# A retrieval layer on one NeuronCore: sixteen more tokens by gathered score rows, another layout of the gate matrix, and work moved between two stages

## The chip, the cores and the metric

The kernel runs on one core of a Trainium2 chip. The metric is the device time of one execution in microseconds (us), as the median of several runs. One execution was profiled; times inside it count from the start of its span.

## The reference

Two layers, each with a mixer (not touched here) and a retrieval layer over 16,384 single-neuron experts, 8 heads with 16 experts each per token, 512 tokens of width 1024:

```
s1 = q[..., :half] . sub_keys[0];  s2 = q[..., half:] . sub_keys[1]
v1, i1 = top_k(s1, 16);  v2, i2 = top_k(s2, 16)
top, pos = top_k(v1[:, None] + v2[None, :], 16)      # 128 experts per token in all
eidx = cidx[pos];  gate = softmax(top)
act  = gelu(sum_d h[t, d] * expert_u[eidx[t, k], d])
y[t] = sum_k gate[t, k] * act[t, k] * expert_v[eidx[t, k], :]
```

## The kernel before

The 512 tokens are four tiles of 128. Three tiles (384 tokens, `DT`) are done densely: all 16,384 experts, in 128 chunks of 128, are scored for these tokens, and a matrix of gates that is zero nearly everywhere picks what counts. The fourth tile is done sparsely: for each of its 128 pairs a row of `peer_u` and one of `peer_v` is gathered per token by an indirect DMA from GpSimd's queue, with a dot product or a multiply-add on VectorE for each.

Of the dense tokens the last `MT` of the first tile in `TILES` are an exception: their columns are left out of the score matmuls, which are `DW = DT - MT` wide. Their scores come from gathered rows too (function `special`), `128 * MT / 128` gathers, each of 128 rows of 4 KB, and they are folded into the gate matrix, while the scores' place in `ga` is filled with ones.

A score chunk is `do_A`: 8 x 3 matmuls (L296 to L298) of the split weights `wh` and `wl` (float32 as a sum of two parts; ScalarE casts `wh`, L268, VectorE makes the remainder `wl`, L277) into one PSUM bank, then Gelu. `do_A` prepares the weights of chunks up to two ahead. The first `AHEAD` chunks are computed before the dense stage and stored in DRAM (`Sd`); the others are computed within it.

Per layer the stages that matter here are these.

- **One-hot stage** (L1106 to L1140): the gate matrix `Gd` is made for 384 tokens in 48 groups of 8 tokens (numbered 0 to 47 here). For a group VectorE writes one-hot rows (`onehots`, L1006 to L1009), TensorE multiplies them (16 matmuls of 128 columns, L1129 and L1130), ScalarE copies the result to `stg`. Every fourth group stores `stg` to `Gd`, 2 MB, from ScalarE's queue. VectorE's other work is spread between the groups: index lookups (`soh` tiles, L1391 to L1400), a step of `special`, and, by a planner, score chunks:

```
def fill(dve, pe=0.0):
    clk[0] += dve
    clk[1] += pe
    while clk[1] + 2.0 < clk[0] and done[0] < AHEAD - 5:
        do_A()
```

  `clk` holds planned times of VectorE and TensorE; `fill` adds a chunk where TensorE would run dry, up to five short of `AHEAD`. The last five follow after the loop.
- **Dense stage** (L1143 to L1270): per chunk a load of `peer_v`, its split `vh` and `vl` (L1165, L1166), the product of scores and gates (L1170), its split `whi` and `wlo`, and 18 matmuls of 512 columns (`vmul`, L1197 to L1202). Chunks with stored scores and chunks with fresh ones alternate; for the latter a `do_A` runs. The gates of 4 chunks come in one read `gtTrue` or `gtFalse` (old or fresh scores). The gathers of the fourth tile (`gather`, L1204 to L1232) go on beside, at a fixed number of rows per chunk: `u` rows of batch `bt` with `v` rows of batch `bt - 1`, 8 rows per batch.

Each engine's instructions run in the order in which the code issues them.

## Time and profile before

| | us |
|---|---|
| median of 3 runs | 2894.12 |
| lowest and highest run | 2890.52, 2898.0 |
| profiled execution | 2890.39 |
| its span | 2888.4 |
| TensorE matmul busy in the span | 2822.1 (98%) |
| VectorE busy | 2408.6 (83%) |
| ScalarE busy | 1286.3 (45%) |
| GpSimd busy | 950.2 (33%) |

A busy TensorE row says that matmuls were in flight, not that they were issued at the highest rate: they are pipelined, and the distance of two starts tells the rate. Names such as L296 are lines of the kernel before. `pa` and `pb` are PSUM banks, `grow` is a tile of gathered score rows, `row` one of the dense stage.

### The profile page before, as it was taken

To read this page: it belongs to the slowest core of one execution; us is meant where nothing else is said; L and a number is where in the kernel's file an instruction comes from. 1 tells how busy PE (TensorE), PEld (TensorE's weight loads), DVE (VectorE), ACT (ScalarE), POOL (GpSimd) and SP (SyncE) were. 2 spreads that over 40 slices of the span, in tenths; PEclk is the share of its full clock that TensorE was granted. 3 is DMA by queue.
4 is the path that set the end of the run, shared out by engine and by line. 5 is a ranking of instruction groups with operands and counts; after the bars stand their busy time and mean duration, and the time that the engine had idled before them with its cause. 6 is when DMAs were issued, how large, how long until landed. Compare 5 with 4: busy or idle time off the path is not lost. (4 is left out here: it accounts for less than half of the span.)

```text
span 2888.4 us, 41930 instructions
## 1 busy us (share of the span) xinstructions
PE 2822.1 (98%) x15203; PEld 2439.5 (84%) x15203; DVE 2408.6 (83%) x4724; ACT 1286.3 (45%) x2023; POOL 950.2 (33%) x809
## 2 busy tenths in 40 slices
PE   8999999999999999999999999999999999999999
PEld 4667899988888888888866778999888888888888
DVE  7868989978888888888868589899688888888887
ACT  4343466773333333333343434677633333333332
POOL 1424412003444433344323343120034443343442
PEclk9999999999999999999999999999999999999999
DMA  7443368779999999999944323687799999999996
GB/s 270 132 126 95 116 213 310 260 273 360 348 368 365 360 381 339 364 370 363 338 142 128 103 90 112 227 308 265 285 325 356 351 343 350 354 347 354 349 342 234
DMA packets 320272, 802.80 MB, mean 278 GB/s; under 512 B 27744, under 2 KB 157376, under 8 KB 316992
## 3 DMA queue, kind: packets, MB, share of 16 engines
q1 hardware_dynamic: 220144, 440.25, 45.2%
q0 software_dynamic: 78912, 285.41, 26.2%
q10 hardware_dynamic: 21008, 74.46, 6.8%
q8 instruction: 119, 1.95, 0.3%
q14 instruction: 89, 0.73, 0.1%
HBM read 723.42 MB, written 76.60 MB: 277 GB/s over the span
## 5 line engine op out<-in xcount | busy, mean ns | idle before, releaser
L296 PE MATMUL pa<-hh,wh 128*128 128x368 f32 (+1 forms) x2544 | 882.3, 347 | 4.5 <-ACT hh L371 1.9
L298 PE MATMUL pa<-hh,wl 128*128 128x368 f32 (+1 forms) x2544 | 869.4, 342 | 5.1 <-DVE wl L277 5.1
L297 PE MATMUL pa<-hl,wh 128*128 128x368 f32 (+1 forms) x2544 | 869.3, 342 | 3.1 <-DVE hl L364 2.7
L1166 DVE TENSOR_TENSOR vl<-vr,vh 128x1024 fp32r<-128x1024 f32 x256 | 313.3, 1224 | 257.4 <-ACT vh L1165 257.1
L296 PEld LDWEIGHTS pa<-hh,wh 128*128 128x128 f32 x2544 | 480.0, 189 | 43.2 <-issue 7.8
L297 PEld LDWEIGHTS pa<-hl,wh 128*128 128x128 f32 x2544 | 479.8, 189 | 29.3 <-DVE hl L364 4.5
L298 PEld LDWEIGHTS pa<-hh,wl 128*128 128x128 f32 x2544 | 479.0, 188 | 26.6 <-DVE wl L277 6.1
L1215 POOL DMA_INDIRECT row<-in_peer_u_dram,eidx x256 | 325.7, 1272 | 492.7 <-DVE acc L1228 363.8
L1165 ACT CAST vh<-vr 128x1024 fp32r<-128x1024 f32 x256 | 269.5, 1053 | 469.5 <-PE pb L1202 252.7
L1224 POOL DMA_INDIRECT row<-in_peer_v_dram,eidx x256 | 311.4, 1216 | 450.6 <-DVE row L1219 417.4
L268 ACT CAST wh<-wr 128x1024 fp32r<-128x1024 f32 x327 | 345.4, 1057 | 87.9 <-DMA wr<-in_peer_uT_dram 51.2
L277 DVE TENSOR_TENSOR wl<-wr,wh 128x1024 fp32r<-128x1024 f32 x266 | 325.6, 1227 | 33.9 <-PE pa L298 16.6
L1228 DVE SCALAR_TENSOR_TENSOR acc<-row,gw,acc 128x1024 f32<-128x1024 f32 x256 | 327.6, 1280 | 0.1
L1219 DVE SCALAR_TENSOR_TENSOR row<-row,htok 128x1024 f32<-128x1024 f32 x256 | 311.9, 1219 | 0.0
L1197 PE MATMUL pb<-vh,whi 128*128 128x512 f32 x762 | 300.0, 394 | 5.2 <-ACT whi L1174 5.1
L1199 PE MATMUL pb<-vl,whi 128*128 128x512 f32 x762 | 298.8, 392 | 0.0
L1200 PE MATMUL pb<-vl,whi 128*128 128x512 f32 x762 | 298.6, 392 | 0.0
L1202 PE MATMUL pb<-vh,wlo 128*128 128x512 f32 x762 | 297.6, 391 | 0.0
L1198 PE MATMUL pb<-vh,whi 128*128 128x512 f32 x762 | 297.4, 390 | 0.0
L1201 PE MATMUL pb<-vh,wlo 128*128 128x512 f32 x762 | 297.3, 390 | 0.1
L871 ACT ACTIVATE ga<-pa 128x368 f32<-128x368 f32 x256 | 122.6, 479 | 312.9 <-PE pa L298 310.8
L1132 ACT ACTIVATE stg<-pb 128x512 f32<-128x512 f32 x192 | 197.7, 1154 | 38.0 <-PE pb L1130 34.2
(335 smaller groups left out, 3923.8 us busy)
## 6 DMA issues: line engine op xcount, KB each, us to landing
wr<-in_peer_uT_dram SPq DMA_DIRECT2D x256, 512.0 KB, 7.5
vr<-in_peer_v_dram SPq DMA_DIRECT2D x256, 512.0 KB, 6.8
Gd<-stg ACTq DMA_DIRECT2D x24, 2048.0 KB, 8.6
adaw<-in_w_ada_dram SPq DMA_DIRECT2D x80, 512.0 KB, 4.4
gtFalse<-Gd SPq DMA_DIRECT2D x34, 768.0 KB, 12.8
Sd<-ga ACTq DMA_DIRECT2D x120, 192.0 KB, 4.3
gtTrue<-Gd SPq DMA_DIRECT2D x30, 768.0 KB, 10.7
gs<-Sd SPq DMA_DIRECT2D x120, 192.0 KB, 7.4
```

Of the source, the lines that this page charges most:

```text
L268: self.nc.scalar.copy(hi, raw)
L277: (eng or self.nc.vector).tensor_tensor(lo, raw, hi.bitcast(F32), ALU.subtract)
L296: nc.tensor.matmul(ps[:, :width], wh, hh[c][:, :width], start=c == first, stop=False)
L297: nc.tensor.matmul(ps[:, :width], wh, hl[c][:, :width], start=False, stop=False)
L298: nc.tensor.matmul(ps[:, :width], wl, hh[c][:, :width], start=False, stop=c == last)
L1166: nc.vector.tensor_tensor(vl, vr, vh.bitcast(F32), ALU.subtract)
L1197: nc.tensor.matmul(y0, a, vh[:, 0:512], start=f, stop=False)
L1199: nc.tensor.matmul(y0, a, vl[:, 0:512], start=False, stop=False)
L1215: nc.gpsimd.indirect_dma_start(out=r, out_offset=None, in_=A["peer_u"], in_offset=bass.IndirectOffsetOnAxis(ap=eidx[:, kk:kk + 1], axis=0))
L1219: nc.vector.scalar_tensor_tensor(r, r, 1.0, htok, ALU.mult, ALU.mult, accum_out=dots[:, k:k + 1])
L1224: nc.gpsimd.indirect_dma_start(out=r, out_offset=None, in_=A["peer_v"], in_offset=bass.IndirectOffsetOnAxis(ap=eidx[:, kk:kk + 1], axis=0))
L1228: nc.vector.scalar_tensor_tensor(acc, r, wb[bt - 1][:, k:k + 1], acc, ALU.mult, ALU.add)
```

## The change

- `MT` goes from 16 to 32: score matmuls are 352 columns wide instead of 368, and `special` gathers 32 rows instead of 16 per layer, two steps per group instead of one, with the same two buffers `grow`.
- `AHEAD` goes from 60 to 76; the planner's cost of a chunk on TensorE is now worked out from the width (3.84 instead of 4.2).
- `Gd` is stored as `[128, 32, 12, 128]` instead of `[12, 128, 128, 32]`: a read for 4 chunks is one run of 6 KB per partition instead of 12 of 512 bytes, and a store is 32 pieces of 512 bytes per partition instead of one of 16 KB.
- The first `NB0 * KB = 24` score rows of the fourth tile are gathered and multiplied in the one-hot stage (`early`, with three buffers: two `grow` and `H`) instead of the dense stage. For this the fourth tile's lookups move from the third to the second of the one-hot loop's tiles. In the dense stage `u` rows then run three batches ahead of the `v` rows.

```
-AHEAD = 60
-MT = 16
+AHEAD = 76
+MT = 32
+KB = 8
+NB0 = 3
...
-        Gd = self.dp.tile([DT // TB, P, NCHUNK, TB], F32, name=f"Gd{l}", tag="Gd")
+        Gd = self.dp.tile([P, NCHUNK // IG, DT // TB, IG * TB], F32, name=f"Gd{l}", tag="Gd")
...
-                        clk[1] += 4.2
+                        clk[1] += 24 * (DW / 2.4 + 13.3) * 1e-3
...
+                def early():
+                    n = NB0 * KB
+                    rows = []
+                    for k in range(n + 2):
+                        if k < n:
+                            rows.append(u([P, D], F32, "H") if k % 3 == 2 else grow())
+                            urow(k, rows[k])
+                        if k > 1:
+                            udot(k - 2, rows[k - 2])
+                            if (k - 1) % KB == 0:
+                                ugate((k - 1) // KB - 1)
+                            yield
...
-                    if k < 3 and next(spec, 0) is None:
-                        fill(1.3)
+                    for _ in range(2 if (n_ % 2 and NB0 * KB > 20) or MT > 16 else 1):
+                        if next(spec, 0) is None:
+                            fill(1.3)
...
-                        nc.scalar.dma_start(Gd[b0 // TB], stg)
+                        nc.scalar.dma_start(Gd[:, :, b0 // TB], stg.rearrange("p (a i) t -> p a (i t)", i=IG))
...
-                    nc.sync.dma_start(gts[old], Gd[:, :, i:i + IG, :].rearrange("b p i t -> p b i t"))
+                    nc.sync.dma_start(gts[old].rearrange("p b i t -> p b (i t)"), Gd[:, i // IG])
...
-                steps += 2.0 * NPAIR * (1 if i < AHEAD else 2) / (2 * NCHUNK - AHEAD - 6)
+                steps += (2.0 * NPAIR - NB0 * KB) * (1 if i < AHEAD else 2) / (2 * NCHUNK - AHEAD - 6)
```

`urow` issues a gather of one `peer_u` row per token, `udot` is its dot product with the tile's activations (`htok`), `ugate` applies Gelu and the gate to a batch of 8.

**Order, first place.** VectorE in the first part of layer 0's one-hot stage (group 7 of before); `oh` and `oi` are one-hots, `grow` a dot product of a gathered row, `wl` a remainder of the weights of a score chunk. Before:

```order
L1006 TENSOR_TENSOR oh_4070<-iota,ij_3470 128x1024
L1007 TENSOR_TENSOR oi_4071<-iota,ij_3470 128x1024
L1008 TENSOR_TENSOR oh_4070<-oi_4071,gg_3472 128x1024
L1009 TENSOR_TENSOR oh_4070<-oi_4071,gg_3472 128x1024
L1391 TENSOR_TENSOR soh_4076<-iotaA,ab_3282 128x2048
L1393 TENSOR_TENSOR soh_4076<-soh_4076,rep_4010 128x2048
L277 TENSOR_TENSOR wl_4084<-wr_4036,wh_4038 128x1024
L1056 SCALAR_TENSOR_TENSOR grow_4032,sdots_3301<-grow_4032,H_3302 128x1024
L277 TENSOR_TENSOR wl_4142<-wr_4080,wh_4082 128x1024
```

The same engine and stage with the change, a group that has a lookup as well:

```order
L1025 TENSOR_TENSOR oh_4268<-iota,ij_3472 128x1024
L1026 TENSOR_TENSOR oi_4269<-iota,ij_3472 128x1024
L1027 TENSOR_TENSOR oh_4268<-oi_4269,gg_3474 128x1024
L1028 TENSOR_TENSOR oh_4268<-oi_4269,gg_3474 128x1024
L1426 TENSOR_TENSOR soh_4274<-iotaA,ab_3284 128x2048
L1428 TENSOR_TENSOR soh_4274<-soh_4274,rep_4170 128x2048
L279 TENSOR_TENSOR wl_4282<-wr_4234,wh_4236 128x1024
L1075 SCALAR_TENSOR_TENSOR grow_4195,sdots_3303<-grow_4195,H_3304 128x1024
L1075 SCALAR_TENSOR_TENSOR grow_4332,sdots_3303<-grow_4332,H_3304 128x1024
L279 TENSOR_TENSOR wl_4343<-wr_4278,wh_4280 128x1024
```

A second dot has come into the group. In groups 2 to 17 of the change there are 32 dots and 33 remainders; before there were 16 and 24 in groups 2 to 18.

**Order, second place.** VectorE at the end of layer 0's one-hot stage, from the last remainder of the loop on. Before (group 39 and on):

```order
L277 TENSOR_TENSOR wl_6190<-wr_6099,wh_6101 128x1024
L1006 TENSOR_TENSOR oh_6220<-iota,ij_5322 128x1024
L1007 TENSOR_TENSOR oi_6221<-iota,ij_5322 128x1024
L1008 TENSOR_TENSOR oh_6220<-oi_6221,gg_5324 128x1024
L1009 TENSOR_TENSOR oh_6220<-oi_6221,gg_5324 128x1024
L974 TENSOR_SCALAR ef_6226<-sres_908_5784 128x128
L975 TENSOR_TENSOR ef_6226<-ef_6226,sres_948_6040 128x128
L976 CAST eidx_1836<-ef_6226 128x128
```

With the change (group 34 and on; `gdots` and `gwts` are the scores and weights of the fourth tile):

```order
L279 TENSOR_TENSOR wl_6715<-wr_6644,wh_6646 128x1024
L1025 TENSOR_TENSOR oh_6745<-iota,ij_6041 128x1024
L1026 TENSOR_TENSOR oi_6746<-iota,ij_6041 128x1024
L1027 TENSOR_TENSOR oh_6745<-oi_6746,gg_6043 128x1024
L1028 TENSOR_TENSOR oh_6745<-oi_6746,gg_6043 128x1024
L872 SCALAR_TENSOR_TENSOR grow_6704,gdots_1839<-grow_6704,htok_1835 128x1024
L872 SCALAR_TENSOR_TENSOR grow_6707,gdots_1839<-grow_6707,htok_1835 128x1024
L1025 TENSOR_TENSOR oh_6777<-iota,ij_6041 128x1024
L1026 TENSOR_TENSOR oi_6778<-iota,ij_6041 128x1024
L1027 TENSOR_TENSOR oh_6777<-oi_6778,gg_6043 128x1024
L1028 TENSOR_TENSOR oh_6777<-oi_6778,gg_6043 128x1024
```

The last remainder of the loop stands five groups earlier (34 instead of 39), and groups 35 to 40 hold the 12 last of the 24 dots of the fourth tile, two per group. On TensorE the last score chunk of the loop stands behind group 33 (38 before), with 59 chunks in the loop (43 before); seven follow after group 47 before the first value chunk, as before.

## Rows read from the trace of the kernel before

**Rows 1.** Busy time by stretch, with TensorE's granted clock, DMA share and rate.

```profile
...
core 0: us, PE busy (x) PEld busy (x) DVE busy (x) ACT busy (x) POOL busy (x), PEclk, DMA share, GB/s
386.80:620.10 233.30, 223.71 (x1787) 216.33 (x1787) 215.46 (x324) 173.55 (x238) 28.62 (x21) 0.98 0.77 271
...
650.00:1440.00 790.00, 784.70 (x3854) 690.63 (x3853) 676.46 (x905) 296.18 (x468) 319.10 (x251) 1.00 0.99 360
1824.90:2056.20 231.30, 223.03 (x1787) 216.18 (x1787) 215.42 (x325) 173.56 (x238) 28.89 (x21) 0.98 0.77 273
...
2090.00:2880.00 790.00, 790.00 (x3897) 696.96 (x3896) 647.99 (x850) 295.27 (x469) 306.90 (x251) 1.00 0.95 337
...
```

**Rows 2.** TensorE in order of time, dense stage of layer 0.

```profile
...
902.55 0.39 PE L1197 MATMUL pb<-vh,whi 128*128 128x512 f32 x1
...
906.63 0.33 PE L296 MATMUL pa<-hh,wh 128*128 128x368 f32 x1
...
910.62 0.40 PE L1197 MATMUL pb<-vh,whi 128*128 128x512 f32 x1
...
```

**Rows 3.** Waits of TensorE, dense stage of layer 0.

```profile
...
PE pb L1197 <- ACT whi L1174: 5.1, 2, 3.0
```

**Rows 4.** VectorE in order of time, first part of layer 0's one-hot stage.

```profile
...
438.42 1.22 DVE L1391 TENSOR_TENSOR soh<-iotaA,ab 128x2048 f16<-128x2048 f16 x1
...
440.88 1.22 DVE L277 TENSOR_TENSOR wl<-wr,wh 128x1024 fp32r<-128x1024 f32 x1
...
446.83 1.47 DVE L1397 TENSOR_TENSOR soh<-soh 128x1024 f16<-128x1024 f16 x3
...
448.55 1.22 DVE L1056 SCALAR_TENSOR_TENSOR grow<-grow,H 128x1024 f32<-128x1024 f32 x1
...
465.02 0.69 DVE L1006 TENSOR_TENSOR oh<-iota,ij 128x1024 f16<-128x1024 f16 x1
...
467.56 1.22 DVE L1056 SCALAR_TENSOR_TENSOR grow<-grow,H 128x1024 f32<-128x1024 f32 x1
...
468.70 1.22 DVE L277 TENSOR_TENSOR wl<-wr,wh 128x1024 fp32r<-128x1024 f32 x1
...
```

**Rows 5.** VectorE in order of time, end of layer 0's one-hot stage.

```profile
...
599.79 1.22 DVE L277 TENSOR_TENSOR wl<-wr,wh 128x1024 fp32r<-128x1024 f32 x1
600.92 0.69 DVE L1006 TENSOR_TENSOR oh<-iota,ij 128x1024 f16<-128x1024 f16 x1
...
606.85 0.69 DVE L1006 TENSOR_TENSOR oh<-iota,ij 128x1024 f16<-128x1024 f16 x1
...
609.39 0.69 DVE L1006 TENSOR_TENSOR oh<-iota,ij 128x1024 f16<-128x1024 f16 x1
...
```

**Rows 6.** TensorE in order of time, the same groups.

```profile
...
609.52 0.22 PE L1130 MATMUL pb<-oh 128*128 128x128 f16 x1 [0.37 <-DVE oh L1009]
...
610.30 0.22 PE L1130 MATMUL pb<-oh 128*128 128x128 f16 x1
...
```

**Rows 7.** The tile of gathered score rows, whole run.

```profile
...
DMA to landing us min/median/max: 5.9/7.6/13.0
```

**Rows 8.** The same tile, issued from 443 to 444 us.

```profile
...
DMA to landing us min/median/max: 12.6/12.6/12.6
```

**Rows 9.** SyncE's queue in order of time, dense stage of layer 0.

```profile
...
1119.11 0.43 SPq L1156 DMA_DIRECT2D gtTrue<-Gd  x1
1121.24 5.61 SPq L1158 DMA_DIRECT2D vr<-in_peer_v_dram  x1
...
```

**Rows 10.** The gate matrix in DRAM, 620 to 660 us.

```profile
...
L1138 ACTq DMA_DIRECT2D Gd<-stg x1: 327/327/327, 625.7 to 625.7; - x1
L1156 SPq DMA_DIRECT2D gtTrue<-Gd x1: 382/382/382, 634.5 to 634.5; - x1
...
```

**Rows 11.** TensorE in order of time, begin of layer 0's dense stage.

```profile
...
653.22 0.39 PE L1197 MATMUL pb<-vh,whi 128*128 128x512 f32 x1
...
```

**Rows 12.** The page's rate in 40 slices of the span.

```profile
...
GB/s 270 132 126 95 116 213 310 260 273 360 348 368 365 360 381 339 364 370 363 338 142 128 103 90 112 227 308 265 285 325 356 351 343 350 354 347 354 349 342 234
...
```

More of the change, by code (lines that the diff above doesn't have):

```diff
@@ L1110, in peer @@
                             fill(1.8)
-                        elif z == (9 if k == 0 else 11):
+                        elif z == (9 if k == 0 else 13):
                             late = operands(TILES[k + 1], ops[k + 1, 4], ops[k + 1, 8])
-                        elif z == (10 if k == 0 else 12) and late:
+                        elif z == (10 if k == 0 else 14):
                             late()
-                        elif (k, z) == (2, 13):
-                            for _ in spec:
-                                pass
-                            late = operands(TILES[0], ii0, jj0, gv)
-                        elif (k, z) == (2, 14):
-                            late()
+                        elif k == 1 and z in (9, 11):
+                            look = self.lookup(u, ab, If, 3, z // 11)
+                            next(look)
+                        if k == 1 and z in (10, 12):
+                            next(look)
+                            ops[3, z] = next(look)
+                            fill(4.3)
+                        elif (k, z) == (1, 15):
+                            operands(3, ops[3, 10], ops[3, 12])
+                    elif (k, z) == (2, 0):
+                        for _ in spec:
+                            pass
+                        spec = early()
+                    elif (k, z) == (2, 11):
+                        late = operands(TILES[0], ii0, jj0, gv)
+                    elif (k, z) == (2, 12):
+                        late()
                     b0 = tok(k, z)
@@ L1204, in gather @@
             def gather():
[L1205 to L1210 removed]
+                nu = NB - NB0
+                for j in range(NB):
                     for k in range(KB):
[L1212 to L1213 removed]
+                        if j < nu:
+                            kk = (NB0 + j) * KB + k
```

55 lines of the change are left out of this document (28 added, 27 removed).

## The prediction

> **What bounds the kernel now.** I read the busy time by stretch first [rows 1]. In the dense stage of either layer (650 to 1440 us, 2090 to 2880 us) TensorE is busy 784.7 and 790.0 of 790.0 us, VectorE 676.5 and 648.0, and the DMA engines show a share of 0.99 and 0.95. A busy TensorE row can still hide slow issue, so I looked at start times [rows 2]: 18 value matmuls of 512 columns take 906.63 - 902.55 = 4.08 us, 227 ns each, and 24 score matmuls of 368 columns take 910.62 - 906.63 = 3.99 us, 166 ns each, back to back. A dense stage of 128 value chunks and 68 score chunks should then last 128 x 4.08 + 68 x 3.99 = 793.6 us; that is its length, so columns bound it. The waits of TensorE in layer 0's dense stage come to only 5.1 us, in two stalls [rows 3].
>
> The one-hot stage lasts 233.3 and 231.3 us [rows 1]. In it VectorE writes the one-hots of 8 tokens in 2.54 us (467.56 - 465.02, one group), a gathered-row dot product takes 1.14 us to the next start (467.56 to 468.70) [rows 4], and a weight remainder `wl` for a score chunk as much (599.79 to 600.92) [rows 5]. TensorE has 16 short matmuls per group, 0.056 us apart (15 of them start from 609.52 to 610.30 us), 0.9 us in all [rows 6]. The score chunks that are computed ahead fill the rest, until `AHEAD - 5` of them are used up. From then on VectorE alone sets the pace: after the last `wl` at 599.79 us only one-hots follow, 2.54 us per group (606.85 to 609.39) [rows 5], and TensorE idles 2.54 - 0.9 = 1.64 us in each. Six groups are so uncovered, 9.8 us per layer.
>
> **The change, part by part.**
>
> Columns. Each score matmul goes from 368 to 352 columns. Between 368 and 512 columns the start distance grows by (226.7 - 166.3)/144 = 0.42 ns per column, so 16 columns are 6.7 ns, and 2 x 128 x 24 matmuls save 41.2 us. A chunk is then 3.83 us. Bounds: 0 if the distance has a floor near 166 ns, 41.2 us if it is linear; no row shows a floor, so I take the whole.
>
> Work moved ahead. Sixteen more chunks per layer leave the dense stage and enter the one-hot stage. This moves TensorE time and costs none, if it is covered there. The dense stage loses 68 x 3.99 - 52 x 3.83 = 72.2 us, the one-hot stage gains 59 x 3.83 - 43 x 3.99 = 54.4 us; this and the 17 other chunks' columns are the 41.2 us, and not a gain beside them.
>
> The one-hot stage, first part. In groups 2 to 17 VectorE now does two score-row dots instead of one. The order of the change has 33 chunks in these 16 groups: TensorE needs 33 x 3.83 + 16 x 0.9 = 140.8 us, 8.8 per group. VectorE needs 16 x 2.54 + 32 x 1.14 + 33 x 1.14 and three lookup halves of 2.46 + 1.72 us (438.42 to 440.88, 446.83 to 448.55) [rows 4], 127 us, 8.0 per group. The third pace is that of the gathers: two buffers, two rows per group, so a buffer's cycle is landing + 1.14 us of dot + about 0.35 us to the next issue. With the median landing of 7.6 us this is 9.1 us, with the lowest, 5.9, it is 7.4 [rows 7]. TensorE's stock of two prepared chunks (7.7 us) bridges 0.3 us per group. I take 1 us per layer; the upper end follows under the rivals.
>
> The landings that matter are those beside a gate store. A row issued as the 16 KB-per-partition store starts lands after 12.6 us [rows 8], against 5.9 without. The store is now in pieces of 512 bytes. The Trainium skill, page "DMA: Bandwidth & Descriptors", section "Queues, rings and completion order", says that each DMA engine goes round robin over its queues, a packet at a time; by that a gather would wait for short pieces instead of 16 KB ones and the landings beside a store would come near 6 us, so the gather term would be nothing. The excess of 6.7 us in the row agrees with the rule for the long pieces; no row of before shows the short ones.
>
> The one-hot stage, last part. The 59 chunks of the loop are used up at group 33, since the planner's clocks charge two dots per group. The last `wl` stands in group 34. Groups 35 to 46 then are VectorE alone: 12 x 2.54 + 12 dots of the gathered tile x 1.14 + 1.0 of small ones = 45.2 us. TensorE does 12 x 0.9 = 10.8 us in them and has about 3.2 us in hand from the last chunk (in the kernel before, 620.1 - 600.92 = 19.2 us of VectorE time hold 7 x 0.9 of work and 9.8 of idle time). It idles 31.2 us, 21.4 more than now; **two layers: +42.8 us**. The bounds: a TensorE that is one chunk further behind gives 17.6 more per layer, and a lead of nothing 24.6.
>
> In this part three buffers carry two rows per group. At a landing of 6.2 us (near the lowest, since no weights are loaded then) three rows take 6.2 + 1.5 = 7.7 us, so a group 5.1 instead of 4.8 us: six groups, 2 us per layer, **+4 us**. Bounds: 0 at 5.9 us, +15 at 7.6.
>
> What leaves the dense stage. 24 dots (1.14 us) and as many 512 KB gathers per layer go from it, with 16 weight loads; its length shrinks by 9%, so no engine there becomes freer or fuller by much. VectorE is not its bound, and the moved dots give nothing back there: that is why their cost in the last part stands alone.
>
> Long reads of the gate matrix. 1536 pieces of 512 bytes per read become 128 of 6 KB. In layer 0 a value load that was issued behind a gate read took 5.61 us to issue at 1121.24 us [rows 9], and late loads delay ScalarE's casts, on which both stalls end. Of the 5.1 us of [rows 3] I take the whole as won, **-5 us**; bounds 0 and -5. The last store and the first reads lie on a chain: store issued at 625.7, first read at 634.5 [rows 10], first value matmul at 653.22 [rows 11]. The store takes 8.8 us of this, and its successor has 18.7 us behind it, while seven score chunks, 27 us, keep TensorE busy. A store that takes half as long again is hidden; cost 0.
>
> Sum: -41.2 + 42.8 + 4 + 2 - 5 = +2.6 us. The profiled execution took 2890.39 us, 2.0 of it outside its span, and stands 3.7 us under the median of the three runs, 2894.12. 2890.4 + 2.6 + 3.7 gives the forecast: **no change, 2897 us**. I count 0.3% (8.7 us) as what can be told from no change.
>
> **The rivals.**
>
> Faster. TensorE enters the last part a chunk further behind, since it and not VectorE paces the first two parts (8.8 against 8.0 us per group in the first): the idle term is 2 x 17.6 = 35 instead of 42.8, and the row waits of both parts vanish: -41.2 + 35.2 - 5 = -11, 2883 us. With two chunks it is -41.2 + 27.4 - 5 = -19, 2875 us. For it: the pace by rows; against: remainders have three buffers, so VectorE can't be far ahead. Chance 0.30.
>
> Slower by the gathers in the first part. If four of 16 groups meet a store and their rows still land in 12.6 us, each lasts 12.6 + 1.5 = 14.1 instead of 8.8 us: 4 x 5.3 = 21 us, less 3 in stock, 18 per layer, 36 in all: 2933 us. It decides from a mean landing of about 7.8 us, where the cycle is 9.3 and the loss 8 us per layer less the stock. For it: landings of up to 13.0 us now [rows 7]; against: the short pieces. Chance 0.14.
>
> Slower by transfers in the dense stage. Layer 0 moves 360 GB/s x 790 us = 284 MB there [rows 1]; 24 rows and 16 weight tiles of 0.52 MB go, 16 x 0.2 MB of stored scores come: 267 MB in 718 us, 371 GB/s. If 360 is all it can have, it lasts 741 us, 23 us more: 2920 us. For it: a share of 0.99 now; against: one slice of the page moved 381 GB/s [rows 12], TensorE hardly waits, and long reads are the cheaper ones. The Trainium skill, same page, section "Specifications", puts the HBM limit of a core at about 358 GB/s, by which the 267 MB would take 746 us, 28 more than the matmuls. The stretch at 360 and the slice at 381 are over it, so here the measurement decides against the rule. Chance 0.10.
>
> Shorter matmuls don't start sooner. Then the 41.2 us are missing: 2938 us. Chance 0.06.
>
> **How the numbers follow.** The forecast has 0.40 (its own range 2886 to 2903), the faster case 0.30, the three slower ones 0.30. Faster than 0.3%, within, slower: 0.30, 0.40, 0.30. The range runs from 2870, the faster case with two chunks and the 5 us by which single runs of before lie apart from the middle one, to 2930, just under the gather case, which leaves out most of two rivals, some 0.15 to 0.2.
>
> **What the profile after would show.** Score matmuls 160 ns apart; a dense stage of about 718 us; TensorE idle 28 to 35 us in the last 12 groups, with no `wl` there; row landings of 6 to 8 us beside a gate store; gate reads that land sooner. Wrong would make me: landings over 9 us in the first part, TensorE waits in layer 0's dense stage, or idle groups that number fewer than twelve.

## The result, and the profile after

The changed kernel takes 2983.38 us (median of 4 runs, 2975.24 to 2985.81) against 2892.32 us (4 runs of before beside it): ratio 1.0307, 95% interval 1.028 to 1.0335. It is slower, where no change was forecast. The profiled execution took 2985.8 us, 95.4 more than that of before; the prediction's sum allowed for 2.6 of it, so 92.8 us are to be found.

Busy time by stretch of the changed kernel, columns as in [rows 1]. First the three parts of layer 0's one-hot stage (groups 2 to 17, 18 to 34, 35 to 46), then the stage as a whole and the dense stage of layer 0, and both of layer 1:

```profile
395.86:558.25 162.39, 154.89 (x1101) 151.74 (x1100) 128.49 (x182) 89.03 (x136) 49.27 (x34) 0.96 0.88 293
558.25:691.26 133.01, 118.75 (x872) 115.81 (x870) 100.86 (x152) 78.17 (x117) 20.70 (x17) 0.95 0.78 264
691.26:741.68 50.42, 23.44 (x180) 18.46 (x181) 45.04 (x76) 27.36 (x33) 10.40 (x9) 0.51 0.73 231
387.40:741.70 354.30, 299.63 (x2173) 288.07 (x2172) 282.73 (x424) 197.10 (x289) 80.88 (x61) 0.89 0.81 269
772.30:1501.40 729.10, 721.41 (x3505) 625.12 (x3504) 639.49 (x846) 275.07 (x421) 279.66 (x227) 1.00 0.97 368
1872.50:2224.40 351.90, 296.33 (x2172) 284.21 (x2172) 282.58 (x423) 197.01 (x289) 83.96 (x61) 0.90 0.81 271
2255.60:2973.90 718.30, 717.26 (x3503) 625.23 (x3504) 604.74 (x783) 273.40 (x419) 279.00 (x227) 1.00 0.94 348
```

The dense stages do what was foretold: 70.6 and 70.8 us shorter than 799.7 and 789.1 us of before (first to last value matmul), forecast 72.2. All of the loss is in the one-hot stage, 354.3 and 351.9 us for 233.3 and 231.3 [rows 1]. By the prediction's own terms it should have lasted 312: 141.8 in the first part (140.8 + 1), 114.9 in the middle (26 chunks x 3.83 + 17 x 0.9), 47.2 in the last (45.2 + 2), 8.5 in groups 0 and 1. Against these the excess (us) is

```
                 forecast   layer 0   layer 1    both layers
groups 2-17        141.8     162.4     163.6        +42.4
groups 18-34       114.9     133.0     128.9        +32.1
groups 35-46        47.2      50.4      51.0         +7.0
dense stage        -72.2     -70.6     -70.8         +3.0
gain of the long reads -5: stalls in layer 0's dense stage not less   +5.0
```

The sum is 89.5; of 92.8 us, 3 have no place here. Two questions are open then: what lengthens the first part, and what the middle.

**The middle part.** All issues of stored scores, in the kernel before and in the changed one (shortest, median and longest in ns), and then ScalarE of the changed kernel in order of time around one gate store (start, duration, and in brackets the idle time before with its releaser):

```profile
L874 ACTq DMA_DIRECT2D Sd<-ga x120: 326/326/356, 340.1 to 2082.5; - x120
```

```profile
L893 ACTq DMA_DIRECT2D Sd<-ga x152: 326/326/10624, 341.1 to 2248.9; - x152
```

```profile
674.05 0.33 ACTq L893 DMA_DIRECT2D Sd<-ga  x1
674.41 0.73 ACTq L1182 DMA_DIRECT2D Gd<-stg  x1
...
678.87 10.13 ACTq L893 DMA_DIRECT2D Sd<-ga  x1
689.04 1.04 ACT L270 CAST wh<-wr 128x1024 fp32r<-128x1024 f32 x1 [10.20 <-DMA wr<-in_peer_uT_dram]
```

A store of scores takes 0.33 us to issue. The one that follows the gate store takes 10.13 us, and the cast `wh` behind it in ScalarE's queue starts when it is through; the view names a weight load as releaser, but the row ahead of it shows what the queue was doing. In the changed kernel 18 of the 152 issues took 3.4 us or more, each the first behind a gate store; in the kernel before the longest of 120 took 0.356 us. I call this the hold. VectorE and TensorE in the middle part both wait for ScalarE (sum in us, times, longest):

```profile
DVE wl L279 <- ACT wh L270: 13.9, 6, 7.1
```

```profile
PE pa L298 <- ACT ga L890: 8.2, 3, 4.6
```

**The first part.** VectorE's waits for rows in groups 2 to 17 of layer 0, before and after, the gathers of the `grow` tile of the changed kernel there, and its VectorE in order of time:

```profile
DVE grow L1056 <- DMA grow<-in_peer_u_dram,eR: 12.2, 4, 4.3
```

```profile
DVE grow L1075 <- DMA grow<-in_peer_u_dram,eR: 29.0, 17, 6.1
```

```profile
L1070 POOL DMA_INDIRECT grow<-in_peer_u_dram,eR x32: 943/1685/1982, 400.1 to 548.0; - x32
...
DMA to landing us min/median/max: 4.4/7.1/10.1
```

```profile
414.40 1.22 DVE L279 TENSOR_TENSOR wl<-wr,wh 128x1024 fp32r<-128x1024 f32 x1
416.36 1.23 DVE L1075 SCALAR_TENSOR_TENSOR grow<-grow,H 128x1024 f32<-128x1024 f32 x1 [0.74 <-DMA grow<-in_peer_u_dram,eR]
...
421.18 1.22 DVE L1426 TENSOR_TENSOR soh<-iotaA,ab 128x2048 f16<-128x2048 f16 x1
...
424.71 1.22 DVE L1075 SCALAR_TENSOR_TENSOR grow<-grow,H 128x1024 f32<-128x1024 f32 x1
```

The landings beside a store are less late: at most 10.1 us, where [rows 7] had 13.0 and [rows 8] 12.6. They are not level with the others: the three rows issued within 3 us of a store's start land after 9.2 to 10.1 us, the median of all is 7.1. VectorE waits for rows 17 times, 29.0 us. The 32 gathers are (548.0 - 400.1)/31 = 4.77 us apart, 9.54 us for two; the prediction's cycle with a landing of 7.1 us gives 7.1 + 1.14 + 0.35 = 8.6. A part of the difference stands in the last three rows. The dot that starts at 424.71 is of a row that GpSimd issued at 414.75 and that landed 6.0 us later, at 420.8; VectorE was at one-hots and a lookup, which its order has first, and came to the row 3.9 us after. Its buffer was free and asked for a new row as much later. That is one of the longer cases: over the 32 rows of the part the turn takes 1.0 us on average, over 0.5 us for 12 rows. So with two buffers a late row makes VectorE wait, and a busy VectorE makes the next row late. The pace makes about 16 x (9.54 - 8.8) = 12 of the 21 us; besides, the rows don't fill the part: the first is issued 4.2 us after its begin, and it ends 10.3 us after the last is issued, 4.2 + 147.9 + 10.3 = 162.4.

**The last part.** The same part of the kernel before by busy time; TensorE's waits of the changed kernel from 691 to 760 us; and the end of its chain from the last gate store to the first value matmul:

```profile
577.49:620.11 42.62, 37.27 (x340) 34.56 (x339) 41.19 (x65) 36.20 (x47) 0.00 (x0) 0.92 0.69 251
```

```profile
PE pb L1172 <- DVE oh L1027: 27.1, 13, 5.5
```

```profile
L1182 ACTq DMA_DIRECT2D Gd<-stg x1: 520/520/520, 747.0 to 747.0; - x1
L1202 SPq DMA_DIRECT2D gtTrue<-Gd x1: 330/330/330, 756.9 to 756.9; - x1
```

```profile
772.31 0.39 PE L1243 MATMUL pb<-vh,whi 128*128 128x512 f32 x1
```

TensorE waits for one-hots, as forecast, and VectorE is busy 45.0 of 50.4 us; TensorE is busy 23.4 us there, 37.3 of 42.6 before. The last store takes 9.9 us to the first read, 8.8 before [rows 10], and the score chunks after the loop cover it: 25.3 us from store to value matmul, 27.5 before [rows 10, 11].

**The dense stage.** Score matmuls of the changed kernel, 24 apart; waits in layer 0's dense stage; loads of `peer_v`; the page's rate:

```profile
667.80 0.32 PE L300 MATMUL pa<-hh,wl 128*128 128x352 f32 x1
...
671.64 0.32 PE L300 MATMUL pa<-hh,wl 128*128 128x352 f32 x1
```

```profile
PE pb L1243 <- ACT whi L1220: 7.7, 7, 2.2
```

```profile
L1204 SPq DMA_DIRECT2D vr<-in_peer_v_dram x256: 327/328/1446, 757.3 to 2960.3; - x128
```

```profile
GB/s 261 134 131 90 118 241 311 255 254 267 361 351 376 371 387 367 386 377 382 337 152 124 92 93 123 258 311 236 285 259 343 351 360 364 364 358 364 355 360 248
```

3.84 us for 24 matmuls (a chunk in the one-hot stage) is 160 ns each, the linear price of 352 columns. Value loads issue in 1.45 us at most, where [rows 9] had 5.61. Slices of up to 387 GB/s, against 381 in [rows 12], carry the denser traffic, and the stalls are 7.7 us instead of 5.1 [rows 3].

### The profile page after: what moved, and what is told of

Same layout as the page of the kernel before. It is cut to its first block, busy times and chain, and to the rows that moved or that the text cites. A ratio compares the mean times of both kernels' runs of the same rounds, so it can differ in the third digit from the quotient of the medians.

```text
span 2983.6 us, 42247 instructions
## 1 busy us (share of the span) xinstructions
PE 2818.7 (94%) x15203; PEld 2427.5 (81%) x15203; DVE 2455.3 (82%) x4788; ACT 1286.5 (43%) x2023; POOL 990.7 (33%) x841
## 5 line engine op out<-in xcount | busy, mean ns | idle before, releaser
L298 PE MATMUL pa<-hh,wh 128*128 128x352 f32 (+1 forms) x2544 | 876.4, 344 | 27.2 <-ACT ga L890 21.4
L300 PE MATMUL pa<-hh,wl 128*128 128x352 f32 (+1 forms) x2544 | 862.2, 339 | 15.0 <-DVE wl L279 15.0
L299 PE MATMUL pa<-hl,wh 128*128 128x352 f32 (+1 forms) x2544 | 865.0, 340 | 3.1 <-DVE hl L366 2.7
L300 PEld LDWEIGHTS pa<-hh,wl 128*128 128x128 f32 x2544 | 486.8, 191 | 38.5 <-DVE wl L279 17.9
L1262 POOL DMA_INDIRECT row<-in_peer_v_dram,eidx x256 | 304.0, 1188 | 571.8 <-DVE row L872 486.2
L867 POOL DMA_INDIRECT row<-in_peer_u_dram,eidx x208 | 266.0, 1279 | 289.3 <-DVE acc L1266 264.0
L1266 DVE SCALAR_TENSOR_TENSOR acc<-row,gwts,acc 128x1024 f32<-128x1024 f32 x256 | 327.5, 1279 | 0.1
L872 DVE SCALAR_TENSOR_TENSOR row<-row,htok 128x1024 f32<-128x1024 f32 x208 | 253.4, 1218 | 0.2 <-DMA row<-in_peer_u_dram,eidx 0.2
L890 ACT ACTIVATE ga<-pa 128x352 f32<-128x352 f32 x256 | 118.8, 464 | 189.2 <-PE pa L300 184.5
## 6 DMA issues: line engine op xcount, KB each, us to landing
gtFalse<-Gd SPq DMA_DIRECT2D x26, 768.0 KB, 10.3
```

Of the source, the lines that this page charges most:

```text
L298: nc.tensor.matmul(ps[:, :width], wh, hh[c][:, :width], start=c == first, stop=False)
L299: nc.tensor.matmul(ps[:, :width], wh, hl[c][:, :width], start=False, stop=False)
L300: nc.tensor.matmul(ps[:, :width], wl, hh[c][:, :width], start=False, stop=c == last)
L1266: nc.vector.scalar_tensor_tensor(acc, r, gw[:, j, k:k + 1], acc, ALU.mult, ALU.add)
```

## Experiments

In all tables a part's length runs from VectorE's first one-hot of its first group to that of the next part (the last part and the one-hot stage end at the first one-hot of group 47). Idle is TensorE's: the sum of the start distances in excess of 227, 166, 160 and 56 ns for matmuls of 512, 368, 352 and 128 columns, so that slow issue counts as idle too. The one-hot column holds groups 0 and 1 as well; the seven or more chunks behind the loop stand in no column. All is worked out from the trace's start times; two numbers are layers 0 and 1, in us. A row is one execution: those of e2, e5, e9 and e17 were 6 to 10 us under the median of their runs.

```
                 one-hot      idle    | 2-17      idle | 18-34     idle | 35-46   idle | dense     idle
before           233.3/231.3  19/17   | 108/105    5/3 |  74/75    2/2  | 43/43  10/10 | 800/789  15/5
the change       354.3/351.9  87/82   | 162/164  16/16 | 133/129  25/22 | 50/51  38/39 | 729/718  16/5
e1               341.6/345.1  72/77   | 163/171  18/21 | 118/115   9/10 | 52/51  40/39 | 754/733  40/19
e2               244.9/250.3  31/36   | 106/108    4/8 |  82/86    8/10 | 49/48  18/18 | 791/789   7/5
e4               332.5/335.3  63/68   | 159/160  13/13 | 113/115   6/8  | 51/52  39/40 | 726/718  13/5
e5               346.1/346.6  31/31   | 160/157  14/10 | 115/114   2/2  | 63/68   9/14 | 711/689  43/21
e6               308.4/307.3  41/38   | 160/159  14/12 | 106/106   5/5  | 34/34  15/15 | 736/722  23/8
e7               298.1/296.4  21/19   | 124/123    7/8 |  98/97    3/3  | 68/68   9/8  | 735/725  14/4
e8               320.3/319.6  53/50   | 146/147    4/4 | 117/116   5/5  | 49/48  37/36 | 736/717  23/4
e9               287.9/289.1  21/22   | 147/147    4/4 |  90/90    2/2  | 42/44   8/9  | 742/720  28/6
e10              272.5/272.5  34/34  | 146/146    4/4 |  87/87    5/5  | 31/31  20/20 | 762/749  17/5
e11              290.1/289.4  21/20  | 147/146    4/4 |  92/92    4/3  | 43/42   8/7  | 741/723  28/9
e12              281.4/281.9  73/75   | 170/171  21/22 |  72/71   27/27 | 31/31  20/20 | 794/779  19/5
e13              279.3/281.7  71/73   | 159/162  42/45 |  81/81    4/3  | 31/31  20/20 | 794/785  19/10
e14              259.4/261.6  51/55   | 147/150    4/4 |  73/73   22/24 | 31/31  20/20 | 797/780  22/5
e15              282.2/280.2  35/37  | 137/138  20/21 |  84/85    5/5  | 52/49   5/3  | 738/721  25/7
e16              319.6/317.8  51/50  | 135/138  16/21 | 107/107  14/12 | 69/64  16/12 | 730/717  16/4
e17              255.6/256.1  10/10   | 104/106    3/3 |  95/96    2/2  | 48/46   5/3  | 737/728  16/8
e18              240.2/241.0  26/27   | 106/106    3/3 |  94/96    2/2  | 31/31  19/20 | 791/790   6/6
```

In the cuts of code `...` marks lines left out; the lines are against the changed kernel, in e2 against the kernel before.

**e1: the change with the gate matrix stored and read as before.**

```
+        Gd = self.dp.tile([DT // TB, P, NCHUNK, TB], F32, name=f"Gd{l}", tag="Gd")
...
+                        nc.scalar.dma_start(Gd[b0 // TB], stg)
...
+                    nc.sync.dma_start(gts[old], Gd[:, :, i:i + IG, :].rearrange("b p i t -> p b i t"))
```

> The change with the gate matrix stored and read as before; all else as changed. Theory A (the store in 512-byte pieces fills ScalarE's DMA queue, so that the next store of scores holds ScalarE for 3.4 to 10.6 us, and its casts come late): these long issues go, the one-hot stage falls from 353 to about 310 us per layer, the run to 2895 to 2915 us. Theory B (the gathers' landings with two rows per group are what stretched the stage): landings beside a store go back to 11 to 13 us, and the run stays at 2960 us or more. Theory C (too few chunks for the last groups): the last 12 groups stay at 50 us, and what is over 2890 is theirs; it agrees with A on the total.

3006.73 us, ratio 1.0427 (1.0387 to 1.0467). The scores' issues in e1, and its dense stage in layer 0:

```profile
L893 ACTq DMA_DIRECT2D Sd<-ga x152: 326/326/362, 341.0 to 2255.1; - x152
```

```profile
760.00:1510.00 750.00, 727.72 (x3489) 621.93 (x3488) 637.01 (x843) 272.86 (x419) 279.60 (x227) 0.99 0.99 357
```

No issue is held, and the middle part falls from 133 and 129 to 118 and 115 us, so the new layout is what holds the queue. The total was missed: it is above even that of the change, since with 76 chunks ahead the old short reads cost the dense stages 24.6 and 14.6 us. Here the long reads are worth far more than 5 us.

**e2: only the new layout, in the kernel before.**

```
-                        nc.scalar.dma_start(Gd[b0 // TB], stg)
+                        nc.scalar.dma_start(Gd[:, :, b0 // TB], stg.rearrange("p (a i) t -> p a (i t)", i=IG))
...
```

> The kernel before with the new gate layout alone. Theory A: stores of scores behind a gate store are issued in 3 to 9 us instead of 0.33, ScalarE's casts are late, and the one-hot stage, in which VectorE and TensorE have little slack, grows by 15 to 40 us per layer: 2920 to 2970 us. Theory B: with one row per group no landing is late, the landings beside a store are shorter, and the run is within 10 us of the kernel before or faster.

2915.52 us, 1.0101 (1.008 to 1.0122). Its scores' issues:

```profile
L874 ACTq DMA_DIRECT2D Sd<-ga x120: 326/326/9247, 340.8 to 2102.3; - x120
```

The hold comes with the layout alone, without more tokens or chunks. The one-hot stages are 12 and 19 us longer, the low end of A's 15 to 40, layer 0's dense stage is 9 shorter, and the total stays just under A's 2920.

**e3: stores of scores on SyncE's queue.**

```
-                    nc.scalar.dma_start(Sd[i], ga)
+                    nc.sync.dma_start(Sd[i], ga)
```

> The change with the stores of scores issued from SyncE's queue instead of ScalarE's; the gate store keeps its 512-byte pieces and ScalarE's queue. Theory A: ScalarE is no longer held, the one-hot stage is about 310 us per layer and the run 2895 to 2925 us (SyncE now waits for the scores before later weight loads, which may cost some). Theory B: nothing about the gathers changes, 2970 us or more.

3265.1 us, 1.1306 (1.1283 to 1.133): neither theory. What SyncE's queue waits for in layer 0:

```profile
SPq L893 <- ACT ga L891: 363.9, 62, 12.0
```

SyncE waits for every chunk's Gelu, and the weight loads of later chunks stand behind it: one-hot stages of 458 and 459 us. It says nothing on the hold.

**e4: the gate store in four stores of 1024 pieces, one per group.**

```
-                        nc.scalar.dma_start(Gd[:, :, b0 // TB], stg.rearrange("p (a i) t -> p a (i t)", i=IG))
+                        for q in range(4):
+                            parts.append(lambda q=q, s=stg, b=b0 // TB: nc.scalar.dma_start(
+                                Gd[:, q * 8:q * 8 + 8, b], s[:, q * 32:q * 32 + 32].rearrange("p (a i) t -> p a (i t)", i=IG)))
+                        parts.pop(0)()
...
```

> The change with each gate store of 4096 pieces cut into four of 1024, one per group of 8 tokens, still 512 bytes a piece and on ScalarE's queue. Theory A, by a queue that holds a limited number of pieces: no quarter fills it, no issue behind it is over 2 us, and the run is 2895 to 2925 us. Theory A': the pieces themselves are slow wherever they are put, and the wait is only cut in four: 2950 us or more. Theory B: 2960 us or more.

2946.45 us, 1.0211 (1.0178 to 1.0244). Scores and gate stores in e4:

```profile
L893 ACTq DMA_DIRECT2D Sd<-ga x152: 325/326/1741, 339.9 to 2211.5; - x152
```

```profile
L1186 ACTq DMA_DIRECT2D Gd<-stg x96: 366/447/5274, 432.7 to 2195.2; - x96
```

The same bytes in the same layout, a quarter at a time: the longest hold of a score store falls from 10.6 to 1.7 us, the middle part to 113 and 115 us, which is the forecast's 115, and of the total 28 us (by the ratios) to 37 us (by the spans, 2983.6 to 2946.4) come back. No issue of scores is over 2 us, as A said, but the total is above A's 2925: the first part is only 3 to 4 us shorter, the last one us longer. The queue is not free either: the 18 long issues of the change hold it some 124 us in all, the 96 quarters of e4 take 61.

**e5: e4 with 88 chunks ahead** (`AHEAD = 88`).

> The kernel with the store in quarters (e4, 2946 us) with 88 instead of 76 chunks ahead. Theory A (the last part is idle because the score chunks are used up): TensorE's idle time in groups 35 to 46 falls from 39 us per layer to under 12, each dense stage is 12 x 3.83 = 46 us shorter, the whole one-hot stage about 15 us longer, so 2 x 31 us are won: about 2885, 2875 to 2900. Theory B (the last part lasts as it does because VectorE is the bound in it, and the extra chunks need VectorE's remainders, 12 x 1.14 us, and weight loads that stand in the gathers' way): 2915 or more, with landings of rows over 8 us. Theory C (the transfers bind the shortened dense stage): dense idle over 20 us in layer 0 and 2920 or more.

2941.07 us, 1.0195 (1.0169 to 1.0221). TensorE's waits in layer 0's dense stage:

```profile
PE pb L1252 <- ACT whi L1229: 22.7, 21, 3.3
```

The last part's idle time goes as A said, 39 to 9 and 14 us, but only 5 us are won. The part is 11 to 16 us longer and the dense stages, though 46 us of matmuls shorter, gain 16 and 30: TensorE's waits there end on ScalarE's casts, and ScalarE's own waits for value loads there grow from 72 us in e4 to 92 (C, with A's first half).

**e6: e4 with 8 early rows instead of 24** (`NB0 = 1`).

> The store in quarters with 8 instead of 24 rows of the gathered tile in the one-hot stage; 16 rows go back to the dense stage. If the moved dots alone make the last part long (A), 16 x 1.14 = 18 us per layer go from it and none come back in the dense stage: 2946 - 36 = 2910. If the rows' return makes the dense stage wait for transfers (B), half or more of that is lost: 2925 to 2946, with dense idle time 8 us or more above e4's 12.8 and 5.0.

2913.17 us, 1.0087 (1.0064 to 1.011): 33 us less than e4, A. The rows' return costs the dense stages 10 and 3.5 us.

**e7: e4 with 16 tokens by gathered rows** (`MT = 16`).

> The store in quarters with 16 instead of 32 tokens by gathered rows, all else as in the change. Columns give back 41 us. If the second row per group costs the first part nothing but the 12.9 us of idle time (A), groups 2 to 17 lose some 8 us of idle time per layer and the total is 2946 + 41 - 16 = 2971, so 32 tokens are the better choice. If 32 rows of VectorE time and landings also delay the whole planned order (B), the one-hot stage is shorter by 20 us per layer or more beyond its columns and the total is 2946 or less.

2890.14 us, 1.0004 (0.9989 to 1.002): far below A, so B. The columns' 41 us are lost again and 56 us are won all the same: the one-hot stage is 34 and 39 us shorter, the first part alone 36 and 37, with 25 chunks in it instead of 33.

**e8: e4 with a third row buffer** (and four instead of five weight tiles, to make room).

```
-WR = 5
+WR = 4
...
-                grow = lambda: u([P, D], F32, "grow", bufs=2)
+                grow = lambda: u([P, D], F32, "grow", bufs=3)
```

> The store in quarters with three instead of two buffers for gathered rows in the one-hot stage, and four instead of five for weight tiles, which makes room for it. If the buffer cycle (landing, dot, next issue) is what VectorE waits for in the first part (A), its 30 us of waits for row landings in layer 0 fall to under 8 and TensorE's idle time in groups 2 to 17 from 13 to 5 us per layer: 2930. If the landings are late by the DMA queue and not by the buffer (B), the waits stay at 20 us or more and the total at 2946. A weight buffer less may cost something by itself: then TensorE's waits end on casts that wait for weight loads.

2931.57 us, 1.0148 (1.0124 to 1.0172), as A said. First part of layer 0 in e8 by busy time, VectorE's waits for rows in that part in e4 and in e8, and the gathers of e8:

```profile
401.42:547.39 145.97, 145.97 (x1066) 144.00 (x1065) 127.70 (x182) 91.25 (x138) 46.99 (x34) 0.99 0.95 325
```

```profile
DVE grow L1075 <- DMA grow<-in_peer_u_dram,eR: 30.0, 17, 6.2
```

```profile
DVE grow L1075 <- DMA grow<-in_peer_u_dram,eR: 10.1, 4, 7.1
```

```profile
L1070 POOL DMA_INDIRECT grow<-in_peer_u_dram,eR x32: 941/1682/1689, 405.5 to 535.1; - x32
...
DMA to landing us min/median/max: 5.0/7.5/9.0
```

The landings are no shorter (median 7.5 us), yet the rows come 4.18 us apart instead of 4.77, the waits fall from 30.0 (e4) to 10.1 us, TensorE is busy throughout and the part lasts 146 and 147 us for a forecast of 141.8. Layer 0's dense stage is 10 us longer than in e4, with a weight tile less.

**e9, e10, e11: no early rows.** e9 is e8 with all 128 rows of the fourth tile in the dense stage; e10 has 68 chunks ahead; e11 issues e9's quarters on SyncE's queue. `lag` puts the `v` rows one batch behind the `u` rows, as in the kernel before.

```
-NB0 = 3
+NB0 = 0
...
+                lag = 1 if NB0 == 0 else 0
+                for j in range(NB + lag):
...
```

> The store in quarters, three row buffers (and four weight tiles) as in e8, and no rows of the gathered tile in the one-hot stage: all 128 go through the dense stage again; 32 tokens and 76 chunks ahead stay. By the terms that the runs have given so far (A): from e6 (2913) the 8 last rows go, 9 us per layer of VectorE time, and the buffer gives back 7 to 10 us per layer, so the one-hot stage is about 285 us, with 15 us or less idle in TensorE, and the kernel 2875, 2865 to 2885, faster than the kernel before. Rival (B): the dense stage, which gets the rows back, waits for transfers: idle over 30 us in layer 0, and the total is 2890 or more.

> As e9, with 68 instead of 76 chunks ahead. If the length of the dense stage is set by its transfers in part (B of e9), fewer chunks ahead ease it and this is faster than e9 by 5 us or more; if TensorE's columns set both stages (A), moving 8 chunks changes nothing and both are within 5 us of each other.

> As e9, with the quarters of the gate store issued on SyncE's queue instead of ScalarE's. Theory A (whoever issues a DMA behind a store of many pieces is held): ScalarE loses its last holds (the quarters' issues summed to 61 us in e4, the longest 5.3), and SyncE, whose loads have two to four tiles in hand, takes them without effect: 0 to 8 us faster than e9. Rival B: weight loads behind a held issue on SyncE come late and TensorE waits for casts: 5 us or more slower than e9, with issues of weight loads over 2 us.

e9 takes 2888.18 us, 1.0006 (0.9995 to 1.0017), e10 2890.81, 1.0015 (1.0006 to 1.0025), e11 2903.91, 1.006 (1.0045 to 1.0075). e9 is level with the kernel before, so A's 2875 was missed by 13 us: the one-hot stage came out as said (288 us), but layer 0's dense stage idles 28 us, twice before's. e10 bears A out (3 us from e9): its dense idle time falls to 17 us, its last part's rises from 8 to 20. In e11 the rival was right. SyncE at the end of layer 0's loop:

```profile
683.03 11.95 SPq L1186 DMA_DIRECT2D Gd<-stg  x8
695.08 9.69 SPq L258 DMA_DIRECT2D wr<-in_peer_uT_dram  x5
```

Eight quarters in a row take 12 us, and the weight loads of the last chunks come behind them; TensorE idles 14 us per layer ahead of the dense stage, 5 to 6 in e9.

**e12: thirty-two tokens alone** (as e1, with 60 chunks ahead and no early rows, two row buffers).

> Of the change only the thirty-two tokens by gathered score rows: 60 chunks ahead, the old layout of the gate store with one store per 32 tokens, all 128 rows of the gathered tile in the dense stage, two row buffers. Theory A: columns give 41 us; in the first part two rows per group cost the 13 us of buffer waits per layer that e4 showed, and VectorE's 18 us of dots per layer lengthen the last part by about as much as chunks are missing there: 2886 - 41 + 26 + 10 = 2881, 2870 to 2895. Theory B (the landings beside the long-piece stores, 12 to 13 us, hit two rows per group): 20 us more per layer in the first part: 2910 or more.

2974.45 us, 1.0303 (1.0283 to 1.0322). The first part of layer 0 in e12 and VectorE's waits over its one-hot stage:

```profile
397.96:568.38 170.42, 158.79 (x1122) 155.53 (x1120) 128.32 (x181) 96.34 (x145) 49.60 (x34) 0.95 0.82 290
```

```profile
DVE grow L1075 <- DMA grow<-in_peer_u_dram,eR: 41.0, 16, 8.4
```

This single part of the change, without the new layout and its hold, costs as much as the whole. B holds for its total and for the waits (41.0 us, with the store's long pieces), but not alone: the chunks are also used up in the first part, and the groups behind it idle 27 + 20 us per layer.

**e13 to e16: the planner's order or the buffers?** e13 is e12, e15 is e9, e16 is e8, each with half the charge per row; e14 is e12 with e8's third buffer.

```
-                            fill(1.3)
+                            fill(0.65)
```

> As e12 (2974 us), but the planner charges VectorE 0.65 instead of 1.3 us per row, so that the first part holds about as many score chunks as in the kernel before (22 instead of 33) and the later groups keep theirs. Theory A (the order is the cost): the idle time of the groups behind the first part, 27 + 20 us per layer, falls to about 15 and the first part, which the rows now pace at 9.5 us per group, is 15 us shorter: one-hot stage 250 us, 2915. Theory B (the row buffers pace the first part, whatever the order): the chunks that leave the first part only turn TensorE's busy time there into idle time; the first part stays at 155 us or more, the later groups are longer by the chunks they get, and the one-hot stage stays over 265: 2945 or more.

> As e12 with a third row buffer (and four weight tiles), old charge. Theory A (order): the first part loses its waits, 17 us per layer, and is then paced by TensorE's 33 chunks; the groups behind it stay dry, idle 27 + 20: 2974 - 34 = 2940. Theory B (buffers): the chunks of the later groups also come back, since they were late and not missing: one-hot stage under 245, 2905 or less.

> As e9 (2888 us; store in quarters, three row buffers, no early rows, 76 ahead), with the charge of 0.65 us. TensorE's columns set the stage already, idle 20 us per layer, 8 of it in the last groups. Theory A: fewer chunks in the first part and more in the last bring the idle time of the last groups to 3 us: 2875 to 2883, faster than before. Rival: the first part gets idle instead, since VectorE's rows pace it at 8 to 8.5 us per group: 2885 to 2900.

> The changed kernel with the store in quarters, three row buffers (e8, 2932 us) and the charge of 0.65 us. Theory A (order): the chunks last into the last part and its idle time falls from 37 to 15 us per layer; VectorE is then the bound over the whole stage (its work there is about 300 us), so the one-hot stage goes from 320 to 305: 2900. Rival B: 2925 or more, since the first part is paced by VectorE and rows at the length it has now.

e13 takes 2977.01 us, 1.0295 (1.0269 to 1.0322): no gain, as B said. The chunks moved back (25 instead of 33 in the first part; middle idle 27 to 4), and the first part, with eight chunks (31 us) less in it, is only 12 and 9 us shorter: 159 and 162 us, 42 and 45 of them idle. Rows and not chunks pace it. e14 takes 2938.29, 1.0167 (1.0143 to 1.019): 36 us less, A's 34; the first part falls from 170 to 147 us and the dry groups stay dry. e15 takes 2914.31, 1.0089 (1.0072 to 1.0107), the rival and worse than it said: idle time moves to the first part, 20 and 21 us, and 13 chunks instead of 7 are left for behind the loop, so that the shorter one-hot stage gains nothing. e16 takes 2929.99, 1.0139 (1.0119 to 1.0159), 2 us from e8: its one-hot stage stays at 320 and 318, which is B by the total and not by B's reason. The last part's idle time falls from 37 to 16 and 12 us, as A said, and as much appears in the first part, which is 9 to 11 us shorter, and in the middle.

**e17, e18: what the other parts are worth with 16 tokens.** e17 is e9 with `MT = 16`; e18 has 16 tokens, 60 ahead, two buffers, no early rows: the kernel before with the layout in quarters and the changed file's planner.

> 16 tokens by gathered rows as before, 76 chunks ahead, the new gate layout stored in quarters, three row buffers (four weight tiles), no early rows. Theory A (TensorE's columns set both stages once rows don't pace the first part, so the total follows its idle time): the 24 dots per layer that e7 has more are off VectorE, the last groups have chunks, and idle time falls from 21 to 12 us per layer: 2870 to 2880, faster than before. Theory B (the dense stage, shorter by 16 chunks, waits for transfers): idle over 25 us in layer 0's dense stage, 2885 to 2900.

> The kernel before with the new gate layout stored in quarters, and the planner's order of the changed file; 60 chunks ahead, 16 tokens, two row buffers, no early rows. The term of the prediction for the long reads (A): 5 us less, all in layer 0's dense stage (its idle time from 15.4 to 6 us as in e2), the one-hot stage within 5 us of before: 2880 to 2885. Theory B (quarters still hold ScalarE's queue, up to 5 us a time): the one-hot stage 5 to 8 us longer per layer, 2888 or more.

e17 takes 2889.95 us, 1.0009 (0.9997 to 1.0021): idle time falls as A said, and the median stays, so neither A's time nor B's wait. Its trace is of a run of 2883.64 us, among the shortest of twelve, so a part of that gain in idle time may be this run's alone. e18 takes 2897.22, 1.0036 (1.0022 to 1.0049). Layer 0's dense idle time falls from 15 to 6 us, the gain that A named; its one-hot stages are 7 and 10 us longer, which B's total fits, but not B's reason: the middle idles 2 us, as before, and the last part 19 and 20 instead of 10. The chunks are spent sooner: the middle part is 20 us longer, the last 12 shorter. The changed file charges a chunk at 4.0 instead of 4.2 us and has the fourth tile's lookups earlier; which of the two does it was not tried.

## Why the prediction was wrong

- **The step that failed first: "I take 1 us per layer" for the first part.** It measured 21 us per layer, 42 in all. The cycle (landing, dot, next issue) left out that a landed row waits for its turn in VectorE's order, 1.0 us on average and 3.9 in the example above; measured, two rows take 9.54 us and not 8.6. The trace of before had such turns to read, 3.2 us on average over the 16 rows of layer 0. And two buffers can't average late and early rows, so VectorE waits 29 us too. e8, e13 and e14 show that the buffers are what paces: a third one takes 13 to 23 us per layer off the part, while an order with eight chunks fewer there (e13) takes off 9 to 12 and gives nothing to the total. The sign "landings over 9 us in the first part" came, for 4 of 32 rows in layer 0. The rival "slower by the gathers in the first part" named the place and a like price (18 per layer), but by landings beside a gate store. Those improved: the Trainium skill's rule in "DMA: Bandwidth & Descriptors", "Queues, rings and completion order", that engines go round their queues packet by packet, agrees so far as the longest landing is 10.1 us and no longer 13.0 (13.5 in the same part of e12, whose store has the long pieces). They didn't come down to the 6 us that the prediction drew from it, and the loss came with them shorter.
- **The second: "A store that takes half as long again is hidden; cost 0."** The store's data are hidden; its pieces are not. A store of 4096 holds ScalarE's queue at the next score store, up to 10.6 us, and the casts behind come late: 32 us over both layers in the middle part, shown by e1, e2 and e4 from three sides. Nothing in the working asked what stands behind the store in the queue that issues it.
- **Long reads, -5 us.** Mis-sized, and on a condition. In the kernel before they are worth 9 us, all in layer 0 (e2, e18); beside 76 chunks ahead 39 (e1), which the change had to spend at once on its denser traffic, so that its stalls are not less than before's. With the short reads (e1) the stretch moved 357 GB/s, idled 40 us and lasted 754: a stall such as the rival on transfers names appears there. That the dense stage came out at the forecast length with this term at 5 us is in part luck.
- **The last part.** Forecast 31.2 us of idle time per layer and 2 of row waits, measured 38 and 39 in a part 3 to 4 us longer than forecast: right in cause, a little small. That extra chunks fill it (e5) holds, but they don't pay, since the dense stage then waits longer.
- **Columns, -41.2, and the dense stage, -72.2 per layer:** right, by 160 ns and 70.6 and 70.8 us. So the rivals of a floor under the matmuls and of transfers at 360 GB/s fall for the kernel as changed; the stretch moved 368. The Trainium skill's 358 GB/s for a core's HBM ("DMA: Bandwidth & Descriptors", "Specifications") is passed again, as the prediction held.
- **"VectorE is not its bound, and the moved dots give nothing back there":** not quite nothing. In e6 the return of 16 rows per layer costs the dense stages 10 and 3.5 us, in e9 that of 24 rows 6 and 2.6 against e8; in exchange e6's one-hot stages are 24 and 28 us shorter than e4's.

By place the first part lost most, 42 us against 32 in the middle. By runs that change one thing the order is not so clear: the quarters (e4) give back 28 to 37 us of the total, by the parts 33 in the middle and 7 in the first; the third buffer on top (e8) gives 15, with 26 off the first parts and some of it lost again in layer 0's dense stage, where there is a weight tile less. Both causes are shown, and their shares only roughly. The last 9 us of the first parts stand in e8 too, where TensorE is busy throughout: it has 33 to 34 chunks there and short stalls, so the forecast's 141.8 was a little low by itself. What makes the hold is open in part: e4 has the same pieces at the same stride, fewer per store, but also spread over four groups, and in e11 eight quarters in a row take 12 us of SyncE's queue. What the tail's last 3 to 4 us per layer are was not tried.

No version beats the kernel before: e7, e9 and e17 are level with it, by different ways. In their traces TensorE's columns plus 57 (e17) to 88 us (e9) of idle time, chunks behind the loop included, are the whole; before it was 66. Of the 41 us of columns that 32 tokens save in e9 against e17, 31 come back as idle time: 12 in groups 0 and 1, 10 in the dense stages, 8 in the last parts. Which waits these are was not tried.

## What to carry to other kernels

A pace by gathered rows is not landing plus use: add the time until the consumer's program order comes to the row, and with two buffers and two rows per round a late row and a busy consumer both cost; a third buffer was the change that helped here. When a transfer is cut into more pieces, look at the next DMA issue in the same queue, and at what computes behind it, before its landing is called hidden. And moving work between two stages that the same engine bounds gained nothing by itself here, however well the idle slots filled (e5, e10).

## What was not expected of the hardware

- The 4096-piece store itself takes 0.5 to 0.7 us to issue; the time shows at the next DMA of that queue (10.13 us at 678.87) and ends about 5.6 us before the store lands (674.41 + 20.2 = 694.6). The Trainium skill, "Perfetto Trace Analysis", "DMA Instruction — HWDGE (DVE, Sync)", has an issue's time in the trace cover a wait for the descriptor generator and the making of its own descriptors. By that the store's own would be made within its 0.73 us; which of the two the 10.13 us of the follower are, no row here shows. Cut in four, the quarters take up to 5.27 us themselves.
- In the last part TensorE was granted 0.51 of its clock, near its 1.2 GHz level, after and during waits for VectorE; before, with nearly twice the matmuls there, 0.92. The short matmuls start 0.107 us apart (median) instead of 0.056, which is some 7 of the 38 us that the table counts as idle; the waits for VectorE are the other 31 (27.1 in the row on the last part, and 4.1 for `oh` of L1028). It cost little, since VectorE paces that part.
- The dense stage took 368 GB/s over 729 us with slices of 387, where before moved 360.
